# A decoder block on one core: turned attention output in the scores' PSUM banks, mixed groups one per unit, two first-layer pieces ahead of each seven products, last sums put off, a narrower warm-up

## The chip, the core and the metric

The kernel runs on one core of a Trainium2 chip. The core's engines work side by side and wait for each other by semaphores: TensorE (PE, matrix products into PSUM; PEld is its loading of the stationary operand), VectorE (DVE), ScalarE (ACT), GpSimd (POOL) and SyncE (SP, which issues the DMAs). The metric is the device time of one execution in microseconds (us), median of the runs.

## The reference

One layer of a decoder block, for 512 rows of 1024 values, in float32:

```python
p = x @ W_in + b_in      # split: u, v (1024 each), q, k (512), v' , r (1024), a_low (16), g_a, g_b (1024)
y_a = gelu(u) * (W_s[g] @ layer_norm(gelu(v)) + b_s)   # per chunk of 128 rows, 8 channel groups g, W_s lower triangular
log_f = log_sigmoid(a_low @ w_gate2 + b_gate) / 16
o = gated linear attention(q, k, v', log_f)            # 4 heads, state carried from chunk to chunk
y_b = o / rms(o per head) * gla_norm_g * silu(r)
m = sigmoid(g_a) * y_a + sigmoid(g_b) * y_b
h = layer_norm(alpha * x + m @ W_out)
out = layer_norm(alpha * h + relu(h @ W_1)**2 @ W_2)   # W_1 1024 x 4096, W_2 4096 x 1024
```

## The kernel before

**Products in three passes.** Each float32 operand a is split into a rounded part (wh, xh, oh and so on, a cast on ACT) and the rest (wl, xl, ol, a subtraction on DVE). A product is then three matmuls: high x high, high x low, low x high. Weights come in pieces of 128 x 1024 values, in the order of `_stream()`: each is loaded by a DMA into a raw buffer, split by `split`, and used by PE. Seven pairs of wh and wl buffers (`W_BUFS`) let pieces be split up to seven ahead of their use; a piece can be split when PE has finished with the piece seven before it. The very last piece of the stream has no such pair: it is split into xh and xl, columns 4 and 5 of 8 (`split_to`, L129), which are free once the last first-layer piece is through.

**Units and slots.** The first half is a row of units on PE, each 24 products (8 steps of the inner dimension, three passes) into one of four banks of the pool ps_m, followed by `pump()`, which runs what `at(n, ...)` planned for slot n. Slots 0 to 7 belong to v, 8 to 15 to u, 16 to 19 to the q and k columns of the second pair of heads, 20 to 27 to v', 28 to 35 to g_a, 36 to 51 to r and g_b in turns (r, r, g_b, g_b), and 52 to 59 to W_out. PE's order is the program's order; up to L808 the order on the other engines is set by the framework's scheduler, from there on (second layer) all but SP follow the program.

**What the slots hold around the change.** The pool ps_a has two banks (tag aux), handed out in turn, and a bank is handed out again when its last reader is done. ps_s has one buffer of two banks (tag sc), for the attention scores (`level_score`, `diag_score`), the last of them in slot 32. `mix(g)` (L656) is one of eight channel groups of y_a: four products pm into an aux bank, mx on DVE, which reads it, and a multiplication into bufA on DVE. Before, each of the four q/k units' `take` makes two groups. `kd_turn` turns half of KD (pt, aux) in slots 17 and 18, and DVE copies it to KD. `gates` (slot 18 for the second pair) makes two products pz (aux, aux), from which ACT and DVE make cum, then POOL, ACT and DVE the operands qt and kt of the second pair's scores, which begin in slot 22. `chunk_out` (products po, aux; L503) makes a chunk's output of one head; two of them stand in each of the slots 29 to 32 and 35 to 38. `r_take` (L712) turns the finished output by four transposes (yt, aux), which DVE reads in t (L718); it stands ahead of the slot's chunk_out.

**Second layer.** W_2's first three quarters are multiplied as 2 x 2 blocks with seven products instead of eight (Strassen's scheme): a pair p has 1024 hidden columns F, of which `operand` takes sums or differences d, splits them into oh and ol, and `seven_products` multiplies them (m, L903) by sums of weight pieces (L126), in the order `ORDER = (2, 6, 3, 7, 4, 1, 5)`; `keep` adds them up in acc, and `together` (L910) combines those. Between the products stand the eight first-layer pieces (f, L612) that make the next pair's F: one ahead of each of the seven, and the eighth ahead of the last product. The operand of product n + 1 is made while product n runs. The last quarter is a plain product of the last F, split into Fs and the first half of xh, xl (`in_parts`), with pieces 136 to 143 of the stream: four blocks of 128 rows, each in two halves (f, L989), then layer norm and the output.

**The start.** While the first DMAs are under way PE runs 15 products of 512 columns of ones (`WARM`, tile idle, which DVE sets).

Of the kernel before, what the change touches and what calls it, by code (L numbers as in the profile page):

```python
# [8 lines left out]
F32 = mybir.dt.float32  # L9
# [28 lines left out]
PAIRS = 3  # L38
ORDER = (2, 6, 3, 7, 4, 1, 5)
LEVELS = (32, 8, 2)  # L40
WARM = (0, 0, 4, 4, 4, 8, 8, 8, 24, 24, 24, 40, 40, 40, 0)
QT_BUFS = 2
DIFF_K = "vector"
DIFF_Q = "gpsimd"
# [5 lines left out]
def hybrid_block(  # L50
# [45 lines left out]
    NB = DF // 512  # L96
    STREAM = _stream()
    NCHUNK = len(STREAM)

    raws, chunks, kept = {}, {}, {}  # L100
    lanes, ring = {0: rpool}, {lane: [] for lane in LANES}
# [25 lines left out]
            state["sum"] = i + 1  # L127

    def split_to(n):  # L129
        while state["split"] < min(n, NCHUNK):  # L130
            i = state["split"]
            load_to(i + 1)
            if i < NCHUNK - 1:
                hi = wpool.tile([P, 1024], F32R, name=f"wh{i}", tag="wh")
                lo = wpool.tile([P, 1024], F32R, name=f"wl{i}", tag="wl")
            else:
                hi, lo = (a[:, 4:6, :].rearrange("p k t -> p (k t)") for a in (xh, xl))
            sum_to(i + 2)
            raw = raws[i][0]
            if i:  # L140
                split(hi, lo, raw)
            chunks[i] = (hi, lo)
            state["split"] = i + 1
        load_to(n + sum(LANES.values()) if 1 in lanes else n + RAW_BUFS)
# [37 lines left out]
    def at(n, *fs):  # L182
        plan.setdefault(n, []).extend(fs)
# [52 lines left out]
        nc.sync.dma_start(xraw[:, k0:k1, :], xT[:, k0:k1, :])  # L236

    wu = ps_a.tile([P, 512], F32, name="wu", tag="aux")
    idle = wpool.tile([P, 1024], F32R, name="idle", tag="wh")
    nc.vector.memset(idle[:, 0:768].bitcast(F32), 1.0)  # L240
    for o in WARM:
        nc.tensor.matmul(wu, idle[:, 0:P], idle[:, P + o : P + 512 + o], start=True, stop=True)

    raw0 = rpool.tile([P, 1024], F32, name="raw0", tag="raw")
    raws[0] = [raw0]
# [404 lines left out]

    at(S_U + 1, mix_bias)

    for e in range(KT):
        col_job(f"u{e}", u_take(e))

    def mix(g):  # L656
        gs = slice(g * P, (g + 1) * P)
        pm = ps_a.tile([P, NCH, P], F32, name=f"pm{g}", tag="aux")
# [10 lines left out]
        )  # L669
        nc.vector.tensor_mul(AT_[:, g, :], AT_[:, g, :], tm)  # L670


    pr1 = Pair()
    pr1.hp = 1
# [3 lines left out]
    for e in range(4):  # L678

        def take(ps, e=e):  # L680
            qk_take(pr1, e, ps)
            mix(2 * e)
            mix(2 * e + 1)

        col_job(f"qk1_{e}", take)
    sgu.close()
    gp1 = pool(gla, "gla_p1", side="left")
    pr1.AT = gp1.tile([P, 2, NCH, P], F32, name="AT1")
    nc.gpsimd.memset(pr1.AT, 0.0)
    pr1.QI = gp1.tile([P, 2, T], F32, name="QI1")  # L690
    pr1.KD = gp1.tile([P, 2, NCH, P], F32, name="KD1")
    pr1.et = gp1.tile([P, 2 * NCH], F32, name="et1")


    def copy_take(half, br):
# [4 lines left out]

    for half in range(2):
        row_unit(xh, xl, copy_take(half, bias_row(C_VG + half * 512)))
    pr0.S, pr1.S = [None, None], [None, None]
    for c in range(NCH):
        for j in range(2):
            at(S_GA + 1 + c, lambda j=j, c=c: chunk_out(pr0, j, c, gp1))
            at(S_R - 1 + c, lambda j=j, c=c: chunk_out(pr1, j, c, gp1))
    for e in range(KT):
        col_job(f"ga{e}", ga_take(e))


    def r_take(e, t1):  # L712
        def f(ps):
            pt = ps_a.tile([P, NCH, P], F32, name=f"yt{e}", tag="aux")
            for c in range(NCH):
                nc.tensor.transpose(pt[:, c, :], bufB[:, c, e * P : (e + 1) * P], ident)
            nc.scalar.activation(t1, ps, AF.Silu, bias=col("r", e))
            nc.vector.scalar_tensor_tensor(  # L718
                t1.rearrange("p (c s) -> p c s", s=P),
                pt,  # L720
                col("gn", e),
                t1.rearrange("p (c s) -> p c s", s=P),
                op0=ALU.mult,
                op1=ALU.mult,
            )

        return f
# [204 lines left out]
    for p in range(PAIRS - 1):  # L932
        F_ = fp.tile([P, 2, 4, T], F32, name=f"F{p + 1}", tag="F")
        jobs = block(take_raw(F_, 0)) + block(take_raw(F_, 1))
        for n, product in enumerate(seven_products(F, p, F_)):
            jobs[n]()
            if n == 6:
                jobs[7]()
            product()
        F = F_  # L940

# [9 lines left out]
        return hi, lo  # L951

    for n, product in enumerate(seven_products(F, PAIRS - 1, None)):
        jobs[n]()
        if n == 6:
            jobs[7]()
            parts.append(in_parts(1, hh[:, 0:4, :], hl[:, 0:4, :]))
        product()
        if ORDER[n] == 4:
            together(7, ((1, 4),))  # L960
            together(4, ((1, 2),), (1, 0))
        if ORDER[n] == 1:
            together(6, ((1, 1), (-1, 2), (1, 3)))
            together(7, ((1, 1),))
        if n == 5:
            Fs = fp.tile([P, 2, 4, T], F32R, name="Fs", tag="F")
# [11 lines left out]
    for t in range(NT):  # L978
# [3 lines left out]
        for pi, (c0, n) in enumerate(pieces):  # L982
# [3 lines left out]
            for f in range(8):  # L986
                (fh, fl), (wh, wl) = parts[f // 4], chunks[u0 + f]
                for i, (s_, m_) in enumerate(passes(fh[:, f % 4, tsl], fl[:, f % 4, tsl], wh[:, sl], wl[:, sl])):
                    nc.tensor.matmul(ps, s_, m_, start=(f == 0 and i == 0), stop=(f == 7 and i == 2))  # L989
            nc.vector.tensor_add(z[:, sl], z[:, sl], ps)  # L990
            nc.vector.bn_stats(st2[t][:, pi, :], z[:, sl])
        mv = lnp.tile([P, 2], F32, name=f"mv_l2{t}", tag="mv", bufs=4)
        rs = lnp.tile([P, 1], F32, name=f"rs_l2{t}", tag="rs", bufs=4)
# [30 lines left out]
def _stream():  # L1024
# [24 lines left out]
    for p in range(PAIRS):  # L1049
        products = [[operand(p, m, h) for h in range(2)] for m in ORDER]  # L1050
        for i, product in enumerate(products):
            out += take(1 + (i == 6)) + product
    out += [("one", 0, None, f2 + 8 * PAIRS + c) for c in range(8 * (DF // 1024 - PAIRS))]
    return out

# [73 lines left out]
```

## Time and profile before

| | |
|---|---|
| median of 3 runs | 775.09 us (774.72 to 777.23) |
| the profiled execution, its own time | 774.76 us |
| its span, first to last instruction | 772.9 us |
| mean granted clock of PE | 0.997 |
| DMA | 85.15 MB, mean 110 GB/s |

The profile is of one execution, and all durations below are of it. Busy times count each instruction from start to end; matmuls overlap, so what one matmul costs PE is the distance to the next one's start. A row of the timeline is: start, length, engine, line of the kernel, operation, out <- in, shape, count, and in brackets the engine's idle time before it with the instruction that ended it. A product of two float32 operands (not split) appears as two matmuls.

### The profile page before, as it was taken

The page shows a single profiled execution, that of the slowest core. Times are in us where ns is not written, and L with a number is a line of the kernel's source. Part 1 is how long each engine was busy: PE and PEld are TensorE (multiplying, and loading weights), DVE is VectorE, ACT ScalarE, POOL GpSimd, SP SyncE. Part 2 cuts the span into 40 slices and gives each one's busy share as a digit, 9 for nine tenths or more (in the row PEclk, how much of TensorE's full clock was granted, in tenths as well). Part 3 has the DMA queues.
Part 4 walks back from the last instruction along what each step waited for, and adds up shares of the span by engine and source line. Part 5 has one row for each costly group of instructions (what it writes and reads, how often), then busy time and mean ns, then how long its engine had stood idle before and what let it go on. Part 6 is the DMA issues. An engine that isn't in the chain of part 4 may idle for free.

```text
span 772.9 us, 8847 instructions
## 1 busy us (share of the span) xinstructions
PE 752.5 (97%) x3495; PEld 627.1 (81%) x3495; DVE 490.8 (64%) x585; ACT 355.9 (46%) x453; POOL 68.5 (9%) x87
## 2 busy tenths in 40 slices
PE   9998999989999999999999999999999999999996
PEld 7887888878888877888888987888888888888785
DVE  6569666658766532444447644774687668869955
ACT  5466864353246543545412444454554445454300
POOL 1015400004202201100001000000000000000011
PEclk9999999999999999999999999999999999999999
DMA  7823332200341141332222422444244424435111
GB/s 278 270 63 119 99 133 82 82 28 27 110 137 56 54 128 50 136 110 82 94 88 105 164 75 89 141 133 148 70 161 139 142 75 142 135 132 163 56 55 54
DMA packets 25609, 85.15 MB, mean 110 GB/s; under 512 B 3104, under 2 KB 3360, under 8 KB 25568
## 3 DMA queue, kind: packets, MB, share of 16 engines
q1 hardware_dynamic: 25568, 84.59, 32.8%
q8 instruction: 27, 0.44, 0.2%
q14 instruction: 14, 0.11, 0.0%
HBM read 82.48 MB, written 2.10 MB: 109 GB/s over the span
## 4 chain that ended last, share of the span: by engine, by line
PE 85%; DVE 7%; ACT 3%; issue 2%; DMA 1%; POOL 0%; SPq 0%; DVEq 0%; POOLq 0%
PE f L612 22%; PE m L903 14%; PE ps L206 13%; PE gb L612 6%; PE r L612 6%; PE f L989 5%; PE u L612 5%; PE ga L612 4%; PE qk L612 3%; PE first L275 2%; DVE wl L93 2%; PE sc L482 2%; DMA raw<-in_w_all 1%; ACT wh L92 1%; PE po L508 1%
## 5 line engine op out<-in xcount | busy, mean ns | idle before, releaser
L93 DVE TENSOR_TENSOR wl<-raw,wh 128x1024 fp32r<-128x1024 f32 x144 | 177.1, 1240 | 146.6 <-ACT wh L92 140.0
L92 ACT CAST wh<-raw 128x1024 fp32r<-128x1024 f32 x144 | 148.8, 1046 | 134.1 <-PE ps L206 34.1
L612 PE MATMUL f<-xh,wh 128*128 128x512 f32 (+1 forms) x288 | 105.4, 366 | 0.0
L612 PE MATMUL f<-xl,wh 128*128 128x512 f32 (+1 forms) x288 | 105.2, 365 | 0.0
L612 PE MATMUL f<-xh,wl 128*128 128x512 f32 (+1 forms) x288 | 105.2, 365 | 0.0
L903 PE MATMUL m<-wh,ol 128*128 128x512 f32 x168 | 65.5, 390 | 0.5 <-DVE ol L93 0.5
L903 PE MATMUL m<-wh,oh 128*128 128x512 f32 x168 | 65.5, 390 | 0.3 <-ACT oh L92 0.3
L903 PE MATMUL m<-wl,oh 128*128 128x512 f32 x168 | 65.4, 389 | 0.0
L612 PEld LDWEIGHTS f<-xl,wh 128*128 128x128 f32 x288 | 54.3, 189 | 8.8
L612 PEld LDWEIGHTS f<-xh,wl 128*128 128x128 f32 x288 | 54.3, 189 | 8.8
L612 PEld LDWEIGHTS f<-xh,wh 128*128 128x128 f32 x288 | 54.3, 189 | 8.7
L206 PE MATMUL ps<-wh,xh 128*128 128x512 f32 x128 | 50.8, 397 | 0.0
L206 PE MATMUL ps<-wh,xl 128*128 128x512 f32 x128 | 49.9, 390 | 0.0
L206 PE MATMUL ps<-wl,xh 128*128 128x512 f32 x128 | 49.8, 389 | 0.0
L832 ACT ACTIVATE F<-f 128x512 f32<-128x512 f32 (+1 forms) x28 | 15.0, 536 | 74.6 <-PE f L612 74.6
L126 DVE TENSOR_TENSOR raw<-raw,raw 128x1024 f32<-128x1024 f32 x30 | 36.6, 1221 | 7.9 <-DMA raw<-in_w_all 7.8
L423 POOL TENSOR_TENSOR qt<-cum 128x768 f32<-128x768 f32 (+2 forms) x18 | 30.2, 1709 | 116.6 <-DVE cum L378 102.8
L903 PEld LDWEIGHTS m<-wh,ol 128*128 128x128 f32 x168 | 31.5, 188 | 7.5 <-DVE ol L93 1.0
L903 PEld LDWEIGHTS m<-wh,oh 128*128 128x128 f32 x168 | 31.5, 188 | 7.2 <-ACT oh L92 0.7
L903 PEld LDWEIGHTS m<-wl,oh 128*128 128x128 f32 x168 | 31.5, 188 | 6.6
L996 POOL TENSOR_TENSOR rs_l<-rs_l,nhalf 128x1 f32<-128x1 f32 x4 | 3.9, 987 | 330.0 <-DVE rs_l L995 330.0
L92 ACT CAST oh<-d 128x1024 fp32r<-128x1024 f32 x15 | 15.7, 1050 | 37.6 <-DVE d L829 37.6
(227 smaller groups left out, 1522.3 us busy)
## 6 DMA issues: line engine op xcount, KB each, us to landing
raw<-in_w_all SPq DMA_DIRECT2D x139, 512.0 KB, 3.3
xr<-in_x SPq DMA_DIRECT2D x8, 256.0 KB, 3.6
out<-bufA SPq DMA_DIRECT2D x8, 256.0 KB, 2.0
bufA<-in_xT SPq DMA_DIRECT2D x3, 512.0 KB, 8.9
brow<-in_b_in SPq DMA_DIRECT2D x4, 256.0 KB, 5.8
g<-in_ln_g SPq DMA_DIRECT2D x2, 512.0 KB, 4.8
b<-in_ln_b SPq DMA_DIRECT2D x2, 512.0 KB, 4.8
bufA<-in_xT SPq DMA_DIRECT2D x2, 256.0 KB, 3.5
```

The source lines that it names most:

```text
L92: nc.scalar.copy(hi, src)
L93: nc.vector.tensor_tensor(lo, src, hi.bitcast(F32), op=ALU.subtract)
L126: nc.vector.tensor_tensor(raw, raw, other[0], op=ALU.add if STREAM[i][0] == "sum" else ALU.subtract)
L206: nc.tensor.matmul(ps, s_, m_, start=(k == 0 and i == 0), stop=(k == KT - 1 and i == 2))
L275: nc.tensor.matmul(first[e], s_, m_[:, k, :], start=(k == 0 and i == 0), stop=(k == KT - 1 and i == 2))
L423: getattr(nc, DIFF_Q).tensor_tensor(qv[:, :, s0 : s0 + n, :], c4[:, :, d:4, :], c4[:, :, 0:n, h - 1 : h].broadcast_to([P, na, n, h]), op=A ...
L482: nc.tensor.matmul(sc[:, c, 0:192], pr.kt[:, jc * P : (jc + 1) * P], pr.qt[:, jc, :], start=True, stop=True)
L508: nc.tensor.matmul(po, pr.AT[:, j, c, :], vs, start=True, stop=(c == 0))
L612: nc.tensor.matmul(ps, s_, m_, start=(k == 0 and i == 0), stop=(k == KT - 1 and i == 2))
L832: nc.scalar.activation(dst, ps, AF.Relu)
L903: nc.tensor.matmul(ps, s_, m_, start=(k == 0 and i == 0), stop=(k == 3 and i == 2))
L989: nc.tensor.matmul(ps, s_, m_, start=(f == 0 and i == 0), stop=(f == 7 and i == 2))
```

## The change

- `r_take` takes its bank from ps_s (tag sc) instead of ps_a.
- `mix` stands in slots 14 to 21, one group each, instead of two in each of the slots 16 to 19. The pool of the second pair (AT1, QI1, KD1, et1), which takes the place of the tiles that mix reads, is therefore opened in slot 21.
- Two first-layer pieces stand ahead of the first of each seven products, and one ahead of each of the others; `_stream()` follows.
- Of the sums at the end (`together`), acc4 += acc2 + alpha h, and acc6 += acc1 - acc2, which only the third and fourth row block need, come behind the first row block's two results.
- The piece that is split into xh, xl is 141 (`ASIDE`) instead of 143, and it is split ahead of 142 and 143.
- The warm-up is nine products of 128 x 128 ones, from a tile that POOL sets anyway; the tile idle and its memset on DVE are gone.

```diff
--- before.py
+++ after.py
@@ -38,7 +38,7 @@
 PAIRS = 3
 ORDER = (2, 6, 3, 7, 4, 1, 5)
 LEVELS = (32, 8, 2)
-WARM = (0, 0, 4, 4, 4, 8, 8, 8, 24, 24, 24, 40, 40, 40, 0)
+WARM = 9
 QT_BUFS = 2
 DIFF_K = "vector"
 DIFF_Q = "gpsimd"
@@ -96,6 +96,7 @@
     NB = DF // 512
     STREAM = _stream()
     NCHUNK = len(STREAM)
+    ASIDE = NCHUNK - 3
 
     raws, chunks, kept = {}, {}, {}
     lanes, ring = {0: rpool}, {lane: [] for lane in LANES}
@@ -127,10 +128,11 @@
             state["sum"] = i + 1
 
     def split_to(n):
+        n += n > ASIDE
         while state["split"] < min(n, NCHUNK):
             i = state["split"]
             load_to(i + 1)
-            if i < NCHUNK - 1:
+            if i != ASIDE:
                 hi = wpool.tile([P, 1024], F32R, name=f"wh{i}", tag="wh")
                 lo = wpool.tile([P, 1024], F32R, name=f"wl{i}", tag="wl")
             else:
@@ -236,10 +238,8 @@
         nc.sync.dma_start(xraw[:, k0:k1, :], xT[:, k0:k1, :])
 
     wu = ps_a.tile([P, 512], F32, name="wu", tag="aux")
-    idle = wpool.tile([P, 1024], F32R, name="idle", tag="wh")
-    nc.vector.memset(idle[:, 0:768].bitcast(F32), 1.0)
-    for o in WARM:
-        nc.tensor.matmul(wu, idle[:, 0:P], idle[:, P + o : P + 512 + o], start=True, stop=True)
+    for i in range(WARM):
+        nc.tensor.matmul(wu[:, :P], ones, ones, start=True, stop=True)
 
     raw0 = rpool.tile([P, 1024], F32, name="raw0", tag="raw")
     raws[0] = [raw0]
@@ -650,9 +650,6 @@
 
     at(S_U + 1, mix_bias)
 
-    for e in range(KT):
-        col_job(f"u{e}", u_take(e))
-
     def mix(g):
         gs = slice(g * P, (g + 1) * P)
         pm = ps_a.tile([P, NCH, P], F32, name=f"pm{g}", tag="aux")
@@ -669,6 +666,11 @@
         )
         nc.vector.tensor_mul(AT_[:, g, :], AT_[:, g, :], tm)
 
+    for g in range(KT):
+        at(S_QK - 2 + g, lambda g=g: mix(g))
+    for e in range(KT):
+        col_job(f"u{e}", u_take(e))
+
 
     pr1 = Pair()
     pr1.hp = 1
@@ -679,17 +681,20 @@
 
         def take(ps, e=e):
             qk_take(pr1, e, ps)
-            mix(2 * e)
-            mix(2 * e + 1)
 
         col_job(f"qk1_{e}", take)
-    sgu.close()
-    gp1 = pool(gla, "gla_p1", side="left")
-    pr1.AT = gp1.tile([P, 2, NCH, P], F32, name="AT1")
-    nc.gpsimd.memset(pr1.AT, 0.0)
-    pr1.QI = gp1.tile([P, 2, T], F32, name="QI1")
-    pr1.KD = gp1.tile([P, 2, NCH, P], F32, name="KD1")
-    pr1.et = gp1.tile([P, 2 * NCH], F32, name="et1")
+    pr1.S = [None, None]
+
+    def second_parts():
+        sgu.close()
+        pr1.pool = gp1 = pool(gla, "gla_p1", side="left")
+        pr1.AT = gp1.tile([P, 2, NCH, P], F32, name="AT1")
+        nc.gpsimd.memset(pr1.AT, 0.0)
+        pr1.QI = gp1.tile([P, 2, T], F32, name="QI1")
+        pr1.KD = gp1.tile([P, 2, NCH, P], F32, name="KD1")
+        pr1.et = gp1.tile([P, 2 * NCH], F32, name="et1")
+
+    at(S_QK + 5, second_parts)
 
 
     def copy_take(half, br):
@@ -700,18 +705,18 @@
 
     for half in range(2):
         row_unit(xh, xl, copy_take(half, bias_row(C_VG + half * 512)))
-    pr0.S, pr1.S = [None, None], [None, None]
+    pr0.S = [None, None]
     for c in range(NCH):
         for j in range(2):
-            at(S_GA + 1 + c, lambda j=j, c=c: chunk_out(pr0, j, c, gp1))
-            at(S_R - 1 + c, lambda j=j, c=c: chunk_out(pr1, j, c, gp1))
+            at(S_GA + 1 + c, lambda j=j, c=c: chunk_out(pr0, j, c, pr1.pool))
+            at(S_R - 1 + c, lambda j=j, c=c: chunk_out(pr1, j, c, pr1.pool))
     for e in range(KT):
         col_job(f"ga{e}", ga_take(e))
 
 
     def r_take(e, t1):
         def f(ps):
-            pt = ps_a.tile([P, NCH, P], F32, name=f"yt{e}", tag="aux")
+            pt = ps_s.tile([P, 2, NCH, P], F32, name=f"yt{e}", tag="sc")[:, 0]
             for c in range(NCH):
                 nc.tensor.transpose(pt[:, c, :], bufB[:, c, e * P : (e + 1) * P], ident)
             nc.scalar.activation(t1, ps, AF.Silu, bias=col("r", e))
@@ -933,9 +938,9 @@
         F_ = fp.tile([P, 2, 4, T], F32, name=f"F{p + 1}", tag="F")
         jobs = block(take_raw(F_, 0)) + block(take_raw(F_, 1))
         for n, product in enumerate(seven_products(F, p, F_)):
-            jobs[n]()
-            if n == 6:
-                jobs[7]()
+            if n == 0:
+                jobs[0]()
+            jobs[n + 1]()
             product()
         F = F_
 
@@ -951,16 +956,16 @@
         return hi, lo
 
     for n, product in enumerate(seven_products(F, PAIRS - 1, None)):
-        jobs[n]()
+        if n == 0:
+            jobs[0]()
+        jobs[n + 1]()
         if n == 6:
-            jobs[7]()
             parts.append(in_parts(1, hh[:, 0:4, :], hl[:, 0:4, :]))
         product()
         if ORDER[n] == 4:
             together(7, ((1, 4),))
-            together(4, ((1, 2),), (1, 0))
         if ORDER[n] == 1:
-            together(6, ((1, 1), (-1, 2), (1, 3)))
+            together(6, ((1, 3),))
             together(7, ((1, 1),))
         if n == 5:
             Fs = fp.tile([P, 2, 4, T], F32R, name="Fs", tag="F")
@@ -988,6 +993,8 @@
                 for i, (s_, m_) in enumerate(passes(fh[:, f % 4, tsl], fl[:, f % 4, tsl], wh[:, sl], wl[:, sl])):
                     nc.tensor.matmul(ps, s_, m_, start=(f == 0 and i == 0), stop=(f == 7 and i == 2))
             nc.vector.tensor_add(z[:, sl], z[:, sl], ps)
+            if t == 0:
+                together(*(((4, ((1, 2),), (1, 0))), (6, ((1, 1), (-1, 2))))[pi])
             nc.vector.bn_stats(st2[t][:, pi, :], z[:, sl])
         mv = lnp.tile([P, 2], F32, name=f"mv_l2{t}", tag="mv", bufs=4)
         rs = lnp.tile([P, 1], F32, name=f"rs_l2{t}", tag="rs", bufs=4)
@@ -1049,7 +1056,7 @@
     for p in range(PAIRS):
         products = [[operand(p, m, h) for h in range(2)] for m in ORDER]
         for i, product in enumerate(products):
-            out += take(1 + (i == 6)) + product
+            out += take(1 + (i == 0)) + product
     out += [("one", 0, None, f2 + 8 * PAIRS + c) for c in range(8 * (DF // 1024 - PAIRS))]
     return out
```

TensorE at the end of slot 18, between the last product of the third q/k unit and the first of the fourth (pm of a mixed group, pt of kd_turn, pz of gates). Before:

```order
L612 MATMUL qk_2_1219<-xh,wl_929 128x512
L660 MATMUL pm_1245<-wst,bufB 128x128 x4
L660 MATMUL pm_1253<-wst,bufB 128x128 x4
L400 MATMUL pt_1_1261<-ident,kd_1155 128x128 x4
L368 MATMUL pz_1270<-a_sb,w2s 128x512
L368 MATMUL pz_1274<-a_sb,w2s 128x512
L612 MATMUL qk_3_1295<-xh,wh_968 128x512
```

Now:

```order
L612 MATMUL qk_2_1211<-xh,wl_921 128x512
L400 MATMUL pt_1_1237<-ident,kd_1147 128x128 x4
L657 MATMUL pm_1243<-wst,bufB 128x128 x4
L368 MATMUL pz_1254<-a_sb,w2s 128x512
L368 MATMUL pz_1258<-a_sb,w2s 128x512
L612 MATMUL qk_3_1279<-xh,wh_960 128x512
```

One mixed group instead of two, and it stands behind pt instead of ahead of it.

VectorE at the same place (KD is the copy of pt, mx reads pm, lf reads pz, wl is a weight piece's low part). Before:

```order
L401 COPY KD_321<-pt_0_1207 128x512
L93 TENSOR_TENSOR wl_1290<-raw_1099,wh_1289 128x1024
L662 SCALAR_TENSOR_TENSOR mx_1250<-pm_1245,cols_sb,mixb 128x512
L662 SCALAR_TENSOR_TENSOR mx_1258<-pm_1253,cols_sb,mixb 128x512
L670 TENSOR_TENSOR bufA<-bufA,mx_1250 128x512
L670 TENSOR_TENSOR bufA<-bufA,mx_1258 128x512
L401 COPY KD_321<-pt_1_1261 128x512
L371 TENSOR_SCALAR lf_1267<-pz_1270,cols_sb 128x512
L371 TENSOR_SCALAR lf_1267<-pz_1274,cols_sb 128x512
```

Now, from the weight piece of slot 17 on:

```order
L93 TENSOR_TENSOR wl_1206<-raw_1067,wh_1205 128x1024
L667 TENSOR_TENSOR bufA<-bufA,mx_1202 128x512
L401 COPY KD_313<-pt_1_1237 128x512
L93 TENSOR_TENSOR wl_1274<-raw_1107,wh_1273 128x1024
L659 SCALAR_TENSOR_TENSOR mx_1248<-pm_1243,cols_sb,mixb 128x512
L371 TENSOR_SCALAR lf_1251<-pz_1254,cols_sb 128x512
L667 TENSOR_TENSOR bufA<-bufA,mx_1248 128x512
L371 TENSOR_SCALAR lf_1251<-pz_1258,cols_sb 128x512
```

The second copy of pt to KD now stands ahead of wl and of the group's mx; mx still stands behind wl.

VectorE at the end of the seven products, from the sums behind product 1 to those behind product 5 (Fs and xl <- Flast are the two halves of the last F; wl and xl <- raw are the last weight pieces). Before:

```order
L913 TENSOR_TENSOR bufB<-bufB 128x2x512
L913 TENSOR_TENSOR bufB<-bufB,acc_3172 128x2x512
L93 TENSOR_TENSOR Fs<-Flast,Fs 128x512 x4
L93 TENSOR_TENSOR wl_5290<-raw_5201,wh_5289 128x1024
L93 TENSOR_TENSOR wl_5323<-raw_5234,wh_5322 128x1024
L93 TENSOR_TENSOR xl<-Flast,xh 128x512 x4
L880 TENSOR_TENSOR acc_3174<-acc_3174,m_5_0_5336 128x512
L93 TENSOR_TENSOR wl_5358<-raw_5246,wh_5357 128x1024
L93 TENSOR_TENSOR wl_5368<-raw_5293,wh_5367 128x1024
L880 TENSOR_TENSOR acc_3174<-acc_3174,m_5_1_5350 128x512
L93 TENSOR_TENSOR xl<-raw_5326,xh 128x1024
L913 TENSOR_TENSOR bufB<-bufB,acc_3174 128x2x512 x2
```

Now, from the split of Fs on:

```order
L93 TENSOR_TENSOR Fs<-Flast,Fs 128x512 x4
L93 TENSOR_TENSOR wl_5311<-raw_5224,wh_5310 128x1024
L93 TENSOR_TENSOR xl<-Flast,xh 128x512 x4
L885 TENSOR_TENSOR acc_3166<-acc_3166,m_5_0_5324 128x512
L93 TENSOR_TENSOR xl<-raw_5257,xh 128x1024
L93 TENSOR_TENSOR wl_5348<-raw_5269,wh_5347 128x1024
L93 TENSOR_TENSOR wl_5358<-raw_5314,wh_5357 128x1024
L885 TENSOR_TENSOR acc_3166<-acc_3166,m_5_1_5338 128x512
L918 TENSOR_TENSOR bufB<-bufB,acc_3166 128x2x512 x2
L920 SCALAR_TENSOR_TENSOR bufB<-bufA,bufB 128x2x512
L995 TENSOR_TENSOR bufB<-bufB,f_0_0_5374 128x512
L918 TENSOR_TENSOR bufB<-bufB,acc_3165 128x2x512
```

One wl fewer stands ahead of the split of xl <- Flast, the piece that goes to xl comes ahead of the last two wl, and the sums of acc4 and acc6 stand around the first result of the last quarter.

## The prediction

> **What bounds the kernel now.** I read the page's busy shares first, then the shares of the chain that ended last, then what TensorE (PE) itself waited for, longest first.
>
> ```profile
> PE 752.5 (97%) x3495; PEld 627.1 (81%) x3495; DVE 490.8 (64%) x585; ACT 355.9 (46%) x453; POOL 68.5 (9%) x87
> PE 85%; DVE 7%; ACT 3%; issue 2%; DMA 1%; POOL 0%; SPq 0%; DVEq 0%; POOLq 0%
> ...
> 486.56 5.44 PE f L612 x24
> ...
> PE po L508 <- DVE t L718: 3.1, 2, 2.0
> PE pt L400 <- DVE mx L662: 2.1, 2, 1.1
> PE pz L368 <- DVE KD L401: 1.3, 1, 1.3
> ```
>
> PE is the bound: 97% busy, 85% of the chain. A unit of 24 products takes 5.44 us, 0.227 us from start to start, and no part of the change takes a product of the model away. So the change can only win where PE stands still. A busy sum hides such places (one product's 0.39 us overlaps the next), so I measure each by the distance between two starts, less what the same step takes without a wait.
>
> **Turned attention output (yt) in the scores' banks.** The third column below is engine and line; the bracket is the idle time before a row and who ended it.
>
> ```profile
> 286.99 0.59 PE L510 MATMUL po<-S,QI 128*128 128x256 f32 x2
> 287.42 0.59 PE L512 MATMUL po<-bufB,KD 128*128 128x256 f32 x2
> 290.07 0.67 PE L508 MATMUL po<-bufB,AT 128*128 128x256 f32 x2 [2.05 <-DVE t L718]
> 298.20 0.59 PE L512 MATMUL po<-bufB,KD 128*128 128x256 f32 x2
> 299.89 0.70 PE L508 MATMUL po<-bufB,AT 128*128 128x256 f32 x2 [1.09 <-DVE t L718]
> ```
>
> In these two slots yt, po and po share two aux banks, so the second po waits until VectorE (DVE) has read yt in t L718. The steps take 2.65 and 1.69 us; the same step without a wait, from 286.99 to 287.42, takes 0.43. With yt in the sc tile, whose last reader is four slots back, the po pairs find the banks of the slot before, read one unit (5.44 us) ago. Gain 2.22 + 1.26 = **3.5 us** (bounds 3.1, the bare waits, and 3.7). What is late next is the next yt, which must wait for t of this one; t was read by 290.07, some 4 us behind its unit, and a unit of 5.44 lies between.
>
> **Mixed groups one per unit.** These are PE rows of slots 17 and 18, the table by stretches (busy PE, PEld, DVE, ACT, POOL, then the granted clock), and what stands ahead of the waits.
>
> ```profile
> 148.42 1.95 PE L660 MATMUL pm<-wst,bufB 128*128 128x128 f32 x16
> 151.42 0.66 PE L400 MATMUL pt<-ident,kd 128*128 128x128 f32 x4 [1.05 <-DVE mx L662]
> 157.40 1.95 PE L660 MATMUL pm<-wst,bufB 128*128 128x128 f32 x16
> 160.39 0.66 PE L400 MATMUL pt<-ident,kd 128*128 128x128 f32 x4 [1.04 <-DVE mx L662]
> 161.05 0.50 PE L368 MATMUL pz<-a_sb,w2s 128*128 128x512 f32 x1
> 162.85 0.50 PE L368 MATMUL pz<-a_sb,w2s 128*128 128x512 f32 x1 [1.30 <-DVE KD L401]
> ...
> 143.90:147.30 3.40, 3.40 (x17) 2.81 (x16) 3.37 (x5) 0.00 (x0) 0.00 (x0) 1.00 0.15 59
> 159.60:163.00 3.40, 1.31 (x6) 0.76 (x7) 3.40 (x7) 0.69 (x1) 0.00 (x0) 1.00 0.46 157
> 163.00:166.40 3.40, 3.40 (x9) 2.64 (x10) 1.20 (x2) 2.98 (x3) 0.00 (x0) 0.56 0.02 5
> 288.00:291.40 3.40, 1.35 (x8) 1.23 (x7) 1.54 (x3) 1.97 (x5) 0.74 (x2) 1.00 0.51 154
> ...
> 157.37 1.04 ACT L92 CAST wh<-raw 128x1024 fp32r<-128x1024 f32 x1 [7.93 <-PE qk L612]
> 158.45 1.23 DVE L93 TENSOR_TENSOR wl<-raw,wh 128x1024 fp32r<-128x1024 f32 x1 [4.63 <-ACT wh L92]
> 159.59 1.40 DVE L662 SCALAR_TENSOR_TENSOR mx<-pm,cols_sb,mixb 128x512 f32<-128x512 f32 x2
> 162.11 0.68 DVE L401 COPY KD<-pt 128x512 f32<-128x512 f32 x1
> ```
>
> Two groups (16 rows: 1.95 busy, less the 0.25 by which one product overlaps the next, so 1.7 us) fill both aux banks; pt behind them waits for mx. From pm to pt is 3.00 and 2.99 us: 1.3 lost each time. From pz to pz is 1.80 instead of 0.23: 1.57 lost. Then the clock drops: 3.4 us at 0.56, which costs 3.40 x 0.44 = 1.5 us. Together 5.7 us. A group's own products cost the same wherever they stand.
>
> With one group per slot the order in slot 18 is pt, pm, pz, pz. Pt finds its bank read a slot ago. The first pz wants pt's bank: pt about 0.45 and the KD copy 0.68, while pm's half of 1.7 runs, so next to nothing. The second pz wants pm's bank, that is mx of this group, and DVE has wl ahead of mx, which waits for the cast wh, which waits for the unit's end. From that end: cast 1.04, then KD copy and wl (1.23) to about 2.6, mx 0.7: pz at about 3.4 us. PE's own work to there is pt 0.45 (0.66, less that overlap), pm 0.85 and pz 0.25, so 1.55. So a **new wait of about 1.8 us** takes the place of 4.2 us of waits (bounds 0, if mx came first, and 2.5, if wl came late as well). Behind that pz stands all of unit 19. The other groups stand behind readers a unit old. Four more slots get a switch between narrow and wide products; for one I take 0.1 (bounds 0 and 0.15, the extra in the spacing of a unit's first products), 0.4 in all. If the clock holds, the gain is 5.7 - 1.8 - 0.4 = **3.5 us** (bounds 2.0, clock drop again, and 5.3).
>
> The first half-clock stretch follows 3.40 us with PE busy for 1.31; at 288 us PE was busy for 1.35 of 3.40 and the clock stayed at 1.00. In the new slot 18 I count 1.8 idle in 3.4, busier than either, so the likeliest is no drop. [...]
>
> **Two pieces ahead of the products.** Only the first seven products gain, since F's last piece stands directly ahead of them.
>
> ```profile
> 479.31 0.39 PE L612 MATMUL f<-xh,wl 128*128 128x512 f32 x1
> 480.02 0.50 PE L903 MATMUL m<-wh,oh 128*128 128x512 f32 x1 [0.32 <-ACT oh L92]
> 480.36 0.40 PE L903 MATMUL m<-wl,oh 128*128 128x512 f32 x1
> 481.28 0.50 PE L903 MATMUL m<-wh,ol 128*128 128x512 f32 x1 [0.52 <-DVE ol L93]
> ```
>
> Steps of 0.71 and 0.92 against 0.227: 1.17 us. With a second unit (5.44 us) ahead, oh and ol are ready 5 us early: gain **1.2 us** (bounds 0.8 and 1.2). Later sevens lose nothing, since the seventh product and two pieces still lie behind the operand that they start with. Each slot still issues one weight load, one or two sums and the same splits; the pieces are split seven ahead.
>
> **Last sums put off, piece 141 aside.** At the end DVE is behind.
>
> ```profile
> 698.31 1.23 DVE L913 TENSOR_TENSOR bufB<-bufB 128x1024 f32<-128x1024 f32 x1
> ...
> 725.06 0.51 PE L989 MATMUL f<-wl,xh 128*128 128x512 f32 x1 [0.17 <-DVE wl L93]
> 725.64 0.40 PE L989 MATMUL f<-xh 128*128 128x512 f32 x1
> 726.79 0.50 PE L989 MATMUL f<-xl,xh 128*128 128x512 f32 x1 [0.76 <-DVE xl L93]
> ...
> 743.92 0.69 DVE L990 TENSOR_TENSOR bufB<-bufB,f 128x512 f32<-128x512 f32 x1 [4.02 <-PE f L989]
> ```
>
> PE takes 1.15 us from 725.64 to 726.79 instead of 0.23, 0.92 lost, and waits 0.17 at 725.06: 1.1 us, with a little more for the restart. Four of these sums (4 x 1.2 us) go behind the first results, and one wl split less stands between m1's sums and the split of the last first-layer piece. DVE should reach the last wl about half a microsecond before PE wants it: gain **1.1 us** (bounds 0 and 1.3). The sums put off lie beside the 21 us of the second and third row blocks, where DVE idles 4.0 us ahead of this row alone, once in each block of 10.9 us; uncovered they would cost 4.9 us.
>
> **Warm-up.** Nine narrow products in place of fifteen wide ones.
>
> ```profile
> 1.77 5.85 PE L242 MATMUL wu<-idle 128*128 128x512 f32 x15 [1.77 <-DVE idle L240]
> 4.92 2.70 PE L242 MATMUL wu<-idle 128*128 128x512 f32 x8
> 4.45 0.43 DVE L263 CAST wh<-raw 128x512 fp32r<-128x512 f32 x1 [2.73 <-DMA raw<-in_w_all]
> 13.63 0.50 PE L275 MATMUL first<-xh,wl 128*128 128x512 f32 x1
> ```
>
> The first seven wide ones took 3.15 us, 0.45 each; the last eight, to 7.46, 0.32: a half rate until some 4.6 us after the start, though the clock column says 1.00. Then 26 first products run before the one at 13.63, which waited for wl. That wait is the floor. Now wh is there at 4.88, so PE may begin 2.5 us earlier, slow: at 0.45 until 9.5 us 10 are done, and 16 more at 0.227 end at 13.2. Lost: 0; I take **0.1** (bounds 0 and 3.0, if all 26 run at 0.45). [...]
>
> **The second pair's scores.** Between pz and the first score PE has about 1 us less to do (the half-clock stretch goes), while DVE gets mx and bufA of two groups into this chain.
>
> ```profile
> 186.53 2.83 DVE L441 TENSOR_TENSOR qt<-qt,q 128x512 f32<-128x512 f32 x5
> 188.40 1.46 PE L482 MATMUL sc<-qt,kt 128*128 128x192 f32 x8
> ```
>
> The qt products that this score needs were done about 0.8 us ahead of it. POOL no longer clears AT inside the chain, which gives some of that back. I take 0.3 us lost (bounds 0 and 2).
>
> **Sum.** 3.5 + 3.5 + 1.2 + 1.1 - 0.1 - 0.3 = 8.9 us. The profiled execution took 774.76 us, 0.33 under the median of the runs, 775.09; so 765.9 against its own time, 766.2 against the median. I say 766.0, on its own between 764 and 767.5.
>
> **Rivals.** (1) The clock drops at slot 18 again: speaks for it that 1.31 busy was enough for a drop, against it the 288 us row; 766.0 + 1.5 = 767.5, chance 0.16. (2) The chain to the second pair's scores ends last, with DVE behind by mx and bufA of two groups, 1.3 to 2 us: 767.7, chance 0.10. (3) The start stays at the half rate for twice 4.6 us: by 14.1 us 20 are done, 6 more end at 15.5, 1.9 past the floor: 767.9, chance 0.06. (4) The gains don't reach the end, since splitting weights (wh, wl) becomes the bound behind a denser PE: 773.5, within 0.3%; against it DVE at 64%, chance 0.03. (5) On the other side: narrow groups standing alone, eight slots instead of four, each bring a half-clock stretch at 1.5 us. Eight cost 12 us: 766.0 + 12 = 778. It decides from six such stretches on. Against it: two groups at 140.5 us, without a wait behind them, left the clock at 1.00 (row of 143.90). Chance 0.04. The forecast keeps 0.61.
>
> **The numbers.** 0.3% (2.3 us) is about what a measurement of this kernel tells from no change. Faster by more: forecast and rivals 1 to 3, 0.93; within: 0.03; slower: 0.04. The low end is the sum with no new wait in slot 18 and none at the scores, less the upper bounds elsewhere: 763.2. The high end takes rivals 1 and 2 together: 769.2. Left out are rivals 4 and 5 and the far end of 3.
>
> **What would show it.** Right: no wait of po for t; the stretch of pm, pt, pz between units 18 and 19 about 3.5 us long with one wait, now for mx; clock 1.00 through 140 to 170 us; m L903 without a wait; f L989 starts 0.23 apart; the product that waits for wl still at about 13.6 us. Wrong: a clock under 1.00 there, a wait of sc for qt, kt or AT near 180 us, a new wait of yt, or first products past 14 us.

## The result, and the profile after

| | before | after |
|---|---|---|
| median of 5 runs | 775.03 us (774.57 to 777.23) | **766.69 us** (766.11 to 766.79) |
| profiled execution, its own time | 774.76 us | 766.69 us |
| its span | 772.9 us | 764.8 us |

The ratio is 0.9887 (95% interval 0.9872 to 0.9902): faster by 1.1%. The forecast was 766.0, its own range 764 to 767.5.

First the page of the changed kernel: busy shares, and the shares of the chain that ended last. Then its table of PE's waits (in all, times, longest).

```profile
PE 750.0 (98%) x3498; PEld 626.9 (82%) x3498; DVE 490.2 (64%) x584; ACT 355.6 (46%) x453; POOL 69.6 (9%) x87
...
PE 85%; DVE 6%; ACT 3%; issue 3%; POOL 2%; DMA 1%; DVEq 0%; SPq 0%; POOLq 0%
```

```profile
PE sc L482 <- DVE qt L441: 2.1, 1, 2.1
PE pz L368 <- DVE mx L659: 1.3, 1, 1.3
...
PE sc L482 <- DVE AT L494: 1.0, 2, 0.6
...
PE f L994 <- DVE xl L93: 0.5, 1, 0.5
...
PE f L994 <- DVE wl L93: 0.3, 2, 0.2
```

The waits of po for t, of pt for mx, of pz for KD and of m for oh and ol are gone from the table. The new wait of pz for mx is there as forecast. The waits of the last quarter (f, for xl and wl) hardly shrank: 0.8 us in all, against 0.9 before, where the forecast had them gone. The scores wait for AT twice instead of once.

To see where the time went I set the same products side by side in both traces (PE starts, us):

| product | before | after | gained up to there |
|---|---|---|---|
| score in slot 12 | 122.10 | 122.27 | -0.17 |
| first score of the second pair, slot 22 | 188.40 | 184.36 | 4.04 |
| second score of the second pair, slot 23 | 195.15 | 191.70 | 3.45 |
| its last score, slot 32 | 233.04 | 229.70 | 3.34 |
| last turn of h (pturn) | 437.05 | 430.08 | 6.97 |
| first product of the last quarter | 720.32 | 712.13 | 8.19 |
| last product | 765.67 | 757.55 | 8.12 |

Start -0.2; mixed groups with the second pair's scores 3.5; yt 3.6; two pieces ahead 1.2; last sums -0.1. The sum is 8.1, and the profiled executions differ by 774.76 - 766.69 = 8.07.

Slot 18 in the timeline of the changed kernel, on PE and on DVE, and two stretches of it (busy PE, PEld, DVE, ACT, POOL, then the granted clock):

```profile
156.33 0.60 PE L400 MATMUL pt<-ident,kd 128*128 128x128 f32 x4
156.77 1.06 PE L657 MATMUL pm<-wst,bufB 128*128 128x128 f32 x8
157.72 0.50 PE L368 MATMUL pz<-a_sb,w2s 128*128 128x512 f32 x1
159.51 0.50 PE L368 MATMUL pz<-a_sb,w2s 128*128 128x512 f32 x1 [1.29 <-DVE mx L659]
```

```profile
157.58 1.22 DVE L93 TENSOR_TENSOR wl<-raw,wh 128x1024 fp32r<-128x1024 f32 x1
158.71 0.74 DVE L659 SCALAR_TENSOR_TENSOR mx<-pm,cols_sb,mixb 128x512 f32<-128x512 f32 x1
```

```profile
156.20:159.60 3.40, 2.11 (x16) 1.62 (x14) 2.63 (x4) 2.32 (x3) 0.00 (x0) 1.00 0.01 2
159.60:163.00 3.40, 3.40 (x15) 2.81 (x16) 1.86 (x3) 2.92 (x3) 0.00 (x0) 1.00 0.44 159
```

From pz to pz is 1.79 us, so 1.56 lost (forecast 1.8): mx stands behind wl on DVE. The clock stays at 1.00.

The second slot of yt in the same timeline (yt at 291.29, the pair of po behind it without a bracket, hence without a wait):

```profile
291.29 0.60 PE L721 MATMUL yt<-ident,bufB 128*128 128x128 f32 x4
291.73 0.60 PE L508 MATMUL po<-bufB,AT 128*128 128x256 f32 x2
...
293.02 0.59 PE L508 MATMUL po<-bufB,AT 128*128 128x256 f32 x2
```

And the end. The timeline of before shows the last product of the last first-layer piece and the split of Fs; behind it the timeline of after shows the same two, and the waits of the last quarter:

```profile
714.65 0.39 PE L612 MATMUL f<-xh,wl 128*128 128x512 f32 x1
...
714.97 2.49 DVE L93 TENSOR_TENSOR Fs<-Flast,Fs 128x512 fp32r<-128x512 f32 x4
```

```profile
706.46 0.39 PE L612 MATMUL f<-xh,wl 128*128 128x512 f32 x1
...
716.42 0.50 PE L994 MATMUL f<-xl,xh 128*128 128x512 f32 x1 [0.51 <-DVE xl L93]
...
717.55 0.50 PE L994 MATMUL f<-wl,xh 128*128 128x512 f32 x1 [0.16 <-DVE wl L93]
...
718.69 0.50 PE L994 MATMUL f<-wl,xh 128*128 128x512 f32 x1 [0.17 <-DVE wl L93]
...
708.59 2.49 DVE L93 TENSOR_TENSOR Fs<-Flast,Fs 128x512 fp32r<-128x512 f32 x4
```

Four sums (4.9 us) went from DVE's way, and yet it begins the split of Fs later, measured from that last piece: 714.97 - 714.65 = 0.32 us before, 708.59 - 706.46 = 2.13 after. That is where the experiments begin.

### The profile page after: what moved, and what is told of

It is laid out like the page before. It is cut to its first block, busy times and chain, and to the rows that moved or that the text cites. A ratio compares the mean times of both kernels' runs of the same rounds, so it can differ in the third digit from the quotient of the medians.

```text
span 764.8 us, 8846 instructions
## 1 busy us (share of the span) xinstructions
PE 750.0 (98%) x3498; PEld 626.9 (82%) x3498; DVE 490.2 (64%) x584; ACT 355.6 (46%) x453; POOL 69.6 (9%) x87
## 4 chain that ended last, share of the span: by engine, by line
PE 85%; DVE 6%; ACT 3%; issue 3%; POOL 2%; DMA 1%; DVEq 0%; SPq 0%; POOLq 0%
PE f L612 23%; PE m L908 14%; PE ps L208 10%; PE r L612 6%; PE gb L612 6%; PE f L994 5%; PE u L612 5%; PE ga L612 4%; PE first L275 3%; PE qk L612 2%; PE sc L482 1%; DVE wl L93 1%; POOL qt L423 1%; PE po L508 1%; DVE qt L441 1%
```

## The experiments

Each kernel was timed against the kernel before in five rounds; "us" are medians. All but the first start from the changed kernel (766.7 us).

**1 to 3: the end.** Theory A: two pieces ahead leave only one piece between the last two products, so the sums behind product 1 come nearer to the last first-layer piece and to the last quarter, and that uses up what the put-off sums freed. Theory B: the end waits for raw buffers and casts. The order and the sums make a table of two by two: before (old, old), changed (new, new), and the first two kernels here. The first has the old order in all three pairs, and the stream with it:

```diff
-        if n == 0:
-            jobs[0]()
-        jobs[n + 1]()
+        jobs[n]()
+        if n == 6:
+            jobs[7]()
...
-            out += take(1 + (i == 0)) + product
+            out += take(1 + (i == 6)) + product
```

> The changed kernel (766.7 us) with the order of before: one first-layer piece ahead of each of the seven products and the eighth ahead of the last product, in all three pairs. The sums stay put off and piece 141 stays aside. Theory A (distance): two pieces ahead put the last product 5.4 us closer to the last first-layer piece, and that takes the DVE time that the put-off sums had freed. Then with the old order the waits of PE for xl and wl at the end (1.3 us in the changed kernel) go, and the waits for oh and ol at the first seven products (1.2 us) come back: 766.6 us (766.2 to 767.2), with under 0.4 us of waits of f for DVE behind the seven products. Theory B (loads): the end waits for raw buffers and casts, whatever DVE has to do: the waits at the end stay at 1.1 to 1.4 us and 1.2 us come back at the entrance: 767.9 us (767.5 to 768.3).

The second has the sums at their old places, and piece 143 aside:

```diff
-    ASIDE = NCHUNK - 3
+    ASIDE = NCHUNK - 1
...
             together(7, ((1, 4),))
+            together(4, ((1, 2),), (1, 0))
...
-            together(6, ((1, 3),))
+            together(6, ((1, 1), (-1, 2), (1, 3)))
...
-            if t == 0:
-                together(*(((4, ((1, 2),), (1, 0))), (6, ((1, 1), (-1, 2))))[pi])
```

> The changed kernel with all the sums of acc4 and acc6 back behind the fifth and sixth product, and piece 143 aside as before; two pieces ahead of each seven products stay. Theory A: DVE, already too late by 1.3 us in the changed kernel, has four sums (4.9 us) more ahead of the split of Fs: waits of PE at the end of 4 to 6.5 us, 770 to 772 us. Theory B: waits at the end as they are, 766.7 us (766.3 to 767.1).

The third has the old order in the last pair alone, where it should help, and the new one in the first two, where it gains:

```diff
-            out += take(1 + (i == 0)) + product
+            out += take(1 + (i == (0 if p < PAIRS - 1 else 6))) + product
```

> The changed kernel with the order of before in the last pair alone: two pieces stand ahead of the first product in the first two pairs, and in the last pair the eighth piece stands ahead of the last product. Theory A: the entrance keeps its 1.2 us and the waits at the end go: 765.4 us (765.0 to 766.0), with under 0.4 us of waits of f at the end. Theory B: the end is as it was, 766.7 us (766.4 to 767.1). A third outcome, that the operand of the last pair's first product comes late where only one piece stands between, would show as a wait of m for oh or ol at the start of the last pair and 766.5 us or more.

Measured: old order 766.39 us (ratio 0.9891, 0.9876 to 0.9905), old sums 771.85 (0.9957, 0.9945 to 0.997), old order in the last pair 765.11 (0.9871, 0.9857 to 0.9884). From the first to the last product of the last quarter, which is 45.35 us before and 45.42 in the changed kernel:

| | old sums | sums put off |
|---|---|---|
| old order | 45.35 (before) | 43.71 (experiments 1 and 3) |
| two pieces ahead | 50.15 (experiment 2) | 45.42 (changed) |

The times are those of theory A in all three. Putting the sums off (with the piece set aside, which goes with it in this table and was not tried alone) is worth 1.6 us with the old order and 4.7 with the new; the new order costs 4.8 with the old sums and 1.7 with the sums put off. About 1.7 us of the 4.8 and the 4.7 are a half clock that follows experiment 2's longest wait (3.40 x 0.06 + 3.40 x 0.44, rows below). Theory A had 4 to 6.5 us of waits in experiment 2; in the trace 3.0 us are idle time. First the timeline of the kernel with the old order in the last pair, the last product of the last first-layer piece and the split of Fs; then the same of the kernel with the old sums, with its longest wait, and its stretches there:

```profile
706.91 0.39 PE L612 MATMUL f<-xh,wl 128*128 128x512 f32 x1
...
703.61 2.49 DVE L93 TENSOR_TENSOR Fs<-Flast,Fs 128x512 fp32r<-128x512 f32 x4
```

```profile
706.20 0.39 PE L612 MATMUL f<-xh,wl 128*128 128x512 f32 x1
...
719.77 0.50 PE L995 MATMUL f<-wl,xh 128*128 128x512 f32 x1 [2.81 <-DVE wl L93]
...
711.95 2.49 DVE L93 TENSOR_TENSOR Fs<-Flast,Fs 128x512 fp32r<-128x512 f32 x4
```

```profile
717.40:720.80 3.40, 1.03 (x3) 0.49 (x3) 3.40 (x5) 1.05 (x1) 0.00 (x0) 0.94 0.27 108
720.80:724.20 3.40, 3.31 (x9) 2.11 (x9) 3.40 (x5) 0.00 (x0) 0.00 (x0) 0.56 0.00 0
```

With the old order DVE begins Fs 3.30 us ahead of that product (0.32 behind it before, 2.13 in the changed kernel): Fs stands behind product 1, needs pieces 0 to 3 alone, and two pieces follow there instead of one. No product of the last quarter waits in this trace. With the old sums Fs comes 5.75 us behind it, PE waits 2.81 us for one wl, and the clock behind that falls to 0.56. The entrance into the seven products, the other side of the same edit, is worth 766.39 - 765.11 = 1.3 us.

**4: the warm-up.** The wide warm-up of before in the changed kernel.

> The changed kernel with the warm-up of before (fifteen products of 512 columns from a tile that DVE sets). Theory A: in the changed kernel the first products run at about 0.45 us each until some 10 us, and the 26 ahead of the third pass of the third step end 0.2 to 0.3 us too late; with the wide warm-up wl is the floor again: 766.4 us (766.1 to 766.7), and the first products after the wait for wh 0.3 us or less apart. Rival: what set the start is when the first loads land, which differs from one execution to the next; then the median is the same, 766.7 us (766.5 to 767.0), and the product for wl starts where it did relative to its load.

Measured 766.59 us (0.9891, 0.9875 to 0.9906): 0.1 from the changed kernel, no difference that the runs can tell. The time lies in the ranges of both theories, so it doesn't decide between them. The first rows are the timeline of this kernel, the second that of experiment 1, which has the narrow warm-up:

```profile
7.50 1.07 PE L277 MATMUL first<-xh,wh 128*128 128x512 f32 x4
...
14.32 0.50 PE L277 MATMUL first<-xh,wl 128*128 128x512 f32 x1 [0.53 <-DVE wl L93]
```

```profile
5.10 1.49 PE L275 MATMUL first<-xh,wh 128*128 128x512 f32 x4
...
13.41 0.50 PE L275 MATMUL first<-xh,wl 128*128 128x512 f32 x1 [0.53 <-DVE wl L93]
```

The wide one lets the first product start 2.4 us later and at once at full rate (0.23 apart), the narrow one earlier and at first slow (its first four products take 1.49 us, those of the wide one 1.07); wl comes behind both, and the third pass of the third step waits 0.53 us for it in both, as the rival has it. In the changed kernel's own trace theory A's delay is there: that product starts at 13.95 us without a wait, where the kernel before started it at 13.63 behind one.

**5: yt alone**, in the kernel before:

```diff
-            pt = ps_a.tile([P, NCH, P], F32, name=f"yt{e}", tag="aux")
+            pt = ps_s.tile([P, 2, NCH, P], F32, name=f"yt{e}", tag="sc")[:, 0]
```

> The kernel before (775.0 us) with one line changed: yt takes its bank from the scores' pool. Theory A (banks): the two waits of po for t go, and nothing takes their place: 771.4 us (771.2 to 771.9), between the first and the last of these slots PE is 3.5 to 3.7 us faster. Rival: yt itself now waits for t of the yt ahead of it, or the time comes back at the second layer's entrance: 773 us or more.

Measured 771.17 us (0.995, 0.9933 to 0.9967). From the last score to the last pturn PE takes 433.25 - 232.86 = 200.39 us; before, 437.05 - 233.04 = 204.01. So 3.6 us, as theory A has it (the median lies 0.03 us under its range), and the changed kernel's traces give the same 3.6.

**6: mixed groups as before.**

```diff
-    for g in range(KT):
-        at(S_QK - 2 + g, lambda g=g: mix(g))
...
             qk_take(pr1, e, ps)
+            mix(2 * e)
+            mix(2 * e + 1)
...
-    at(S_QK + 5, second_parts)
+    second_parts()
```

> The changed kernel (766.7 us) with the mixed groups as before, two behind each of the q and k units of the second pair, and the second pair's tiles opened behind them. Theory A: the two waits of pt for mx, that of pz for KD and the half-clock stretch come back (+5.9), the wait of pz for mx goes (-1.6), and the second pair's scores lose nothing (-0.7): about 770.3 us (769.9 to 770.9), granted clock under 0.7 in one stretch of 3.4 us behind slot 18. Rival (clock): if that half-clock stretch was an accident of the one profiled execution, then it is not there and the time is 768.8 us (768.4 to 769.3).

Measured 769.80 us (0.9928, 0.9914 to 0.9943), between the two. The waits of pt and pz are back to the hundredth of a us (1.05, 1.04, 1.30), but the half-clock stretch is not, as the rival has it, though in the stretch from 159.60 to 163.00 PE was busy for even less ahead of it, 1.24 us against 1.31 (its stretches below). What the rival missed is in the timeline: the first score of the second pair now waits, as it did not before.

```profile
159.60:163.00 3.40, 1.24 (x6) 0.61 (x5) 3.40 (x6) 0.69 (x1) 0.00 (x0) 1.00 0.44 157
163.00:166.40 3.40, 3.21 (x14) 2.66 (x15) 1.55 (x3) 2.64 (x3) 0.00 (x0) 1.00 0.02 5
```

```profile
188.03 1.54 PE L482 MATMUL sc<-qt,kt 128*128 128x192 f32 x8 [0.75 <-DVE qt L441]
```

From the second pz to that score: 188.03 - 163.19 = 24.84 us here, 188.40 - 162.85 = 25.55 before, and 24.85 in experiment 5, the kernel before but for yt and without the half clock. So the half-clock stretch, which I priced at 1.5 us, cost 0.7: the rest lay beside the chain from cum to qt, for which PE has to wait anyway. What the mixed groups are worth without it is 769.80 - 766.69 = 3.1 us.

**7 and 8: slot 18 without a group**, and the same with the old order in the last pair. Groups in slots 12 to 16 and 19 to 21, both halves of kd_turn in slot 17 (the last number of the first pair's plan, 18, becomes 17):

```diff
-        at(S_QK - 2 + g, lambda g=g: mix(g))
+        at(S_QK - 4 + g + 2 * (g > 4), lambda g=g: mix(g))
```

> The changed kernel with the eight groups in slots 12 to 16 and 19 to 21, and both halves of kd_turn in slot 17, so that pz finds two free banks in slot 18. Theory A: the wait of pz for mx (1.56 us) was a cost of its own: 765.1 us (764.7 to 765.6), no wait of pz, the first score of the second pair 1.5 us earlier. Rival 1: the chain from cum to the second pair's scores ends last anyway, and sc waits by as much longer: 766.7 us (766.3 to 767.0). Rival 2: groups in slots 12 and 13 delay DVE's work for the first pair's last scores, which then wait: 766 us or more, with a new wait of sc near 105 to 125 us.

> The changed kernel with both edits: the old order in the last pair alone, and no mixed group in slot 18 (groups in slots 12 to 16 and 19 to 21). The two act 500 us apart, so they should add: by theory A for both (1.4 and 1.6 us) 763.7 us (763.2 to 764.3); if the wait in slot 18 only moves to the scores, 765.3 us, as with the order of the last pair alone.

Measured 765.67 us (0.9876, 0.9858 to 0.9893) and 764.02 (0.9855, 0.9837 to 0.9873). The two edits add up (765.11 - 764.02 = 1.1; 766.69 - 765.67 = 1.0), but slot 18 gave 1.0 instead of 1.56: between theory A and rival 1. (A step of 1 us is near what the runs can tell. The intervals of the ratios of 766.69 and 765.67 us overlap; the single times, 766.11 to 766.79 and 765.45 to 765.98, do not.) Rival 2's wait near 105 to 125 us is not there.

```profile
157.95 0.62 PE L368 MATMUL pz<-a_sb,w2s 128*128 128x512 f32 x2
...
183.94 1.54 PE L482 MATMUL sc<-qt,kt 128*128 128x192 f32 x8 [0.84 <-DVE qt L441]
...
179.76 1.50 ACT L435 ACTIVATE qt<-qt 128x1536 f32<-128x1536 f32 x1 [2.48 <-POOL qt L423]
181.15 1.05 ACT L434 ACTIVATE kt<-kt 128x1024 f32<-128x1024 f32 x1
...
182.23 1.23 DVE L436 TENSOR_TENSOR kt<-kt,k 128x1024 f32<-128x1024 f32 x1 [1.19 <-ACT kt L434]
```

These rows are of the timeline of the kernel with slot 18 free. Pz waits for nothing, and sc waits 0.84 us. The ACT and DVE rows show the chain: ACT takes the second level's qt, which waits for POOL, ahead of the kt that this score needs, and DVE waits for that kt. From the first pz to sc are 25.99 us.

**9 and 10: what the score waits for.** In experiment 7's kernel, with a group in slot 19, the scheduler sets mx between lf and cum on DVE, and ACT's second qt ahead of kt. (In the changed kernel that mx stands behind cum, and the second qt ahead of kt too.) Without a group there the scheduler sets qt, kt, qt on ACT. So one kernel has no group in slot 19 (slots 11 to 16, 20 and 21), and the other none behind slot 16 (10 to 15, and two in 16), which shortens the chain alike but takes away PE's work beside it. Both on top of experiment 8; the line of the first, and that of the second:

```diff
-        at(S_QK - 4 + g + 2 * (g > 4), lambda g=g: mix(g))
+        at(S_QK - 5 + g + 3 * (g > 5), lambda g=g: mix(g))
...
-        at(S_QK - 4 + g + 2 * (g > 4), lambda g=g: mix(g))
+        at(min(S_U + 2 + g, S_QK), lambda g=g: mix(g))
```

> The kernel of the two edits (old order in the last pair, slot 18 free; 764.0 us) with the groups in slots 11 to 16, 20 and 21, so that none stands in slot 19. With a group in slot 19 its mx stands on DVE between lf and the scans of cum, and ACT takes the second level's qt, which waits for POOL, ahead of the first level's kt; without it both are gone from the chain to the second pair's first score. Theory A (that chain): about 24 us from pz to what the score needs, against 4 units, two groups and pz, about 23.9 us, on PE: the wait of sc for qt (0.8 us) falls to 0.3 or less, 763.2 us (762.9 to 763.7). Rival: that wait is set by POOL's differences and the exponentials alone, whatever stands on DVE; PE has 0.85 us less beside it, so the wait grows: 764.4 us or more.

> The same with all eight groups ahead of slot 17 (slots 10 to 15 one each, two in slot 16). The chain to the second pair's first score is as short as it gets, no mx and no multiplication of a group stands in it; but PE has only four units and pz beside it, 22.2 us, 2.5 us less than with three groups there. Theory A (chain against cover): the score waits 1 to 1.7 us for qt or kt, 764.3 us (763.9 to 764.9). Rival (DVE's load alone): without the groups DVE is done in time, the wait goes, 763.2 us (762.9 to 763.6).

Measured **763.16 us** (0.9838, 0.9825 to 0.9851) and 764.44 (0.986, 0.9846 to 0.9873). First the timeline of the kernel without a group in slot 19, then that of the one with all groups early:

```profile
158.97 0.62 PE L368 MATMUL pz<-a_sb,w2s 128*128 128x512 f32 x2
...
183.06 1.46 PE L482 MATMUL sc<-qt,kt 128*128 128x192 f32 x8
...
177.07 1.04 ACT L434 ACTIVATE kt<-kt 128x1024 f32<-128x1024 f32 x1
179.66 1.49 ACT L435 ACTIVATE qt<-qt 128x1536 f32<-128x1536 f32 x1 [1.55 <-POOL qt L423]
```

```profile
160.37 0.62 PE L368 MATMUL pz<-a_sb,w2s 128*128 128x512 f32 x2
...
184.34 1.54 PE L482 MATMUL sc<-qt,kt 128*128 128x192 f32 x8 [1.54 <-DVE qt L441]
```

From the first pz to sc are 24.09 us without a wait, and 23.97 with one of 1.54: the chain takes some 24 us, and what decides is whether PE has as much to do beside it. Theory A holds for both, and the rival of DVE's load alone falls: with the least DVE work the score waits longest. What mx and ACT's order each add to the chain was not tried apart. The kernel of 763.16 us beats both kernels, 3.5 us under the changed one.

## Why the prediction was right, and where it was not

- **yt**: 3.5 forecast, 3.6 in two pairs of traces. Banks and readers decide, as the step has it.
- **Mixed groups**: 3.5 forecast, 4.2 up to the first score in the profiled pair. The new wait was 1.56 for 1.8. The term was right in its waits, but wrong to take the half-clock stretch for a property of the kernel: two other kernels with the very same waits (experiments 5 and 6) have none (clock 1.00 from 163.00 to 166.40 us in both), and where it came it cost 0.7, not 1.5. Without it the groups gain 3.1 us to the end, the loss at the scores included. That the number came out is in part luck, for the 4.2 have other parts than the sum's: 2.6 at the two pt as forecast, nothing at pz (its two products are 1.79 us apart, 1.80 before), 0.7 from the clock, and about 0.9 that the sum didn't have. Behind pz now stand three groups instead of two, beside the chain to the scores, where PE has time: the kernel with two groups there (experiment 6) waits 0.75 us for the score. "A group's own products cost the same wherever they stand" was wrong there.
- **Second pair's scores**: -0.3 forecast. In the profiled pair 0.6 was lost between the first and the second score (4.04 to 3.45), at the wait for AT, and another 0.1 by the last: -0.7. Why the score's chain was tight was only guessed; experiments 7 to 10 show it to be the chain of some 24 us, with mx and ACT's order on it, against PE's work beside it.
- **Two pieces ahead**: 1.2 forecast, 1.2 by the landmarks (6.97 to 8.19), 1.3 by experiments 1 and 3. But the step said "Later sevens lose nothing". That was true of PE's waits for oh and ol and false of the end.
- **Last sums**: 1.1 forecast, -0.1 measured. This is the step that failed. "DVE should reach the last wl about half a microsecond before PE wants it" counted what left DVE's queue, and not that the other edit moved the rest of the queue: one first-layer piece (5.44 us on PE) that stood between the last operands and the last quarter now stands ahead of the first product. With the old order in the last pair the same put-off gains 1.6 us, more than forecast. The sums that were put off lie beside the row blocks at no cost, as forecast.
- **Warm-up**: 0.1 lost by the forecast, 0.2 up to slot 12 in the profiled pair, nothing in the medians. The step had PE begin at 4.88 us and wait for wl; in the profiled execution it began at 6.21, behind wh, and reached that product late by itself. Executions of kernels with the same start differ by more: the first score starts at 68.46 us in experiment 2 and at 69.36 in experiment 3.

The total came right within 0.7 us, in part by luck, because misses offset: +0.7 at the mixed groups against -1.2 at the end and -0.4 at the scores. Rivals 1, 3 and 4 did not come. Rival 2 came in a small form. Rival 5 did not: no group alone brought a lower clock (1.00 from 120 to 185 us in the changed kernel).

## What to carry to other kernels

An edit that moves work on the engine that bounds also moves the deadlines of every other engine's queue: two edits to one stretch are to be summed on one time line, not one by one. A wait ahead of a long chain through other engines is worth only what the chain leaves, so ask what the consumer waits for once it is gone, and keep independent work of the bounding engine beside the chain rather than ahead of it. An event seen once in one profile (a stretch at half clock) is a chance, not a term, until other executions show it again.

## What the runs showed of the hardware

The half-clock stretches come and go with the same instructions and the same wait. The first score waits 2.1 us for qt in all twelve traces; in six of them the clock behind it falls (0.56 to 0.74 in the stretch from 68.00 to 71.40 us), in the others it does not (1.00 there). In stretches that start at the same time PE was busy alike: 2.15 us of the 3.40 from 64.60 us on, in the changed kernel as in experiment 5, of which only the latter falls (0.66 from 68.00 to 71.40).

In experiment 5 the half clock holds from 69.06 to 72.47 us. Here are the stretch ahead of it and the half clock itself, and the score's row of the timeline; then the same two stretches in the changed kernel, where that row is 1.54 us long:

```profile
65.65:69.06 3.41, 1.29 (x6) 0.79 (x5) 3.41 (x4) 1.63 (x3) 2.19 (x2) 1.00 0.05 17
69.06:72.47 3.41, 3.41 (x11) 3.21 (x11) 2.80 (x5) 3.08 (x3) 0.40 (x2) 0.50 0.11 23
```

```profile
68.87 2.72 PE L482 MATMUL sc<-qt,kt 128*128 128x192 f32 x8 [2.12 <-DVE qt L441]
```

```profile
65.65:69.06 3.41, 1.29 (x6) 0.78 (x5) 3.41 (x4) 1.63 (x3) 2.19 (x2) 1.00 0.06 24
69.06:72.47 3.41, 3.41 (x18) 3.02 (x18) 2.80 (x5) 3.08 (x3) 0.40 (x2) 1.00 0.13 38
```

PE was busy for 1.29 us of the 3.41 in both, and the clock falls in one. In the kernel before PE was busy for more ahead of the half clock at slot 18, 1.71 us of 3.42:

```profile
159.98:163.40 3.42, 1.71 (x7) 1.09 (x8) 3.42 (x6) 0.70 (x2) 0.00 (x0) 1.00 0.45 153
163.40:166.81 3.41, 3.41 (x9) 2.64 (x8) 0.80 (x2) 3.36 (x4) 0.00 (x0) 0.50 0.02 5
```

In the same trace it was busy for 1.35 of 3.40 from 288.00 us on, and the clock stays at 1.00 there and in the 3.40 us behind. So PE's busy time ahead of a place did not tell by itself whether the clock would fall there. What does tell was not shown: no run was made to test it.

To the second score the half clock costs 0.9 us (77.39 - 68.87 in experiment 5 against 76.49 - 68.87 in the changed kernel), and to the third 0.3 (89.58 against 89.28), since the waits for AT and kt behind it (0.60 and 0.35 us in the changed kernel) are gone from the table of experiment 5.
